# A convolution module whose transfers are put in the source's order

## The chip, the core and the metric

The kernel runs on one core of a Trainium2 chip. The core has engines that run side by side and wait for each other by semaphores: TensorE (PE, matrix products, with its weight loads PEld), VectorE (DVE), ScalarE (ACT), GpSimd (POOL) and SyncE (SP). In this kernel SP issues all transfers between the chip's memory (HBM) and the core's own memory, and 16 DMA engines carry them out. SP runs one instruction stream: a transfer whose wait isn't over holds back all that stand behind it. The metric is the device time of one execution in microseconds, compared by medians.

## What is computed

Two layers of a diffusion trunk for 256 tokens of width 1024, in float32: layer 0 mixes an mLSTM with differential attention and ends in a SwiGLU; layer 1 is a Conformer convolution module and a SwiGLU with 8 experts, of which each token takes 2. The change is in the convolution module:

```
u = modulate(x, mix_pre_g, sh_m, sc_m)
a, g = jnp.split(u @ pw1_w + pw1_b, 2, axis=-1)
h = a * jax.nn.sigmoid(g)
h = depthwise_conv(h, dw_w) + dw_b          # 31 taps along the tokens
h = jax.nn.silu(layernorm(h, ln_g, ln_b))
y = h @ pw2_w + pw2_b
```

## The kernel before

Activations lie channel-major: 1024 channels are 8 tiles k of 128 partitions, with 256 tokens along the free axis. Weights lie in HBM as units of 128 x 2048 floats, 1 MB each. `raw` loads a unit into a ring of six buffers (four `raw`, two `raw2`), and `half` splits half a unit into a rounded part (`whi`, a cast on ACT, L372) and the rest (`wlo`, a subtraction on DVE, L373), since a float32 product is made of three faster ones. `Ahead` runs these halves ahead of the products.

The module runs over four steps `jj`. A step multiplies two pw1 units, `jj` and `4 + jj` (48 matmuls on PE each), which give tiles 2jj and 2jj+1 of a and of g. One step later `glu` makes h of them (two ACT instructions and one DVE product per tile, L1416 to L1418 before, L1420 to L1422 now) and writes it into `hp`, in the traces one of the buffers `B`. From there the tiles go two ways:

- Tiles 0 and 1 (`NV = 2`) are convolved on DVE: `conv_v` is a generator of 31 steps (L1361 and L1364 before, L1365 and L1368 now), of which `fill(n)` puts n at a time between the other DVE work.
- Tiles 2 to 7 are convolved on PE: `conv(k)` makes 64 matmul records of 32 columns of weights, with the tap weights of a pair of tiles (`taps` units, one for tiles 2 and 3, one for 4 and 5, one for 6 and 7) and with `x4`, four copies of the tile, each shifted by one token. `conv_shift(k)` makes the copies: one write of the tile to scratch in HBM (`hd<-B`, L1345) and four shifted reads (`B<-hd`, L1348). There are three `x4` buffers.

The first two convolved tiles, 0 and 2, give a pilot mean on PE (`mm<-B,on`), which is subtracted from every tile before the sums of the layer norm (`aux<-B,one`, `aux<-m,one`). In program order, inside step 3, PE's row is: product of unit 3, conv(2), pilot, sums, product of unit 7, conv(3), conv(4), conv(5), conv(6), conv(7).

A scheduler orders what isn't bound to the source's order. `order = in_order()` (L1422) binds PE, DVE and ACT for the module, but not SP: SP's transfers come in the order in which the scheduler finds their buffers free and their data ready, and loads of later parts (the pw2 units) are taken in between. The kernel's last part, the experts, streams some 270 MB of weights through the same SP queue.

Of the kernel before, what the change touches and what calls it, by code (L numbers as in the profile page):

```python
# [11 lines left out]
F32 = mybir.dt.float32  # L12
# [7 lines left out]
P = 128  # L20
# [11 lines left out]
HW = T + 32  # L32
# [6 lines left out]
NV = 2  # L39
# [197 lines left out]
def build(ctx: ExitStack, tc: tile.TileContext, d, unit, dbg=None):  # L237
    nc = tc.nc
# [5 lines left out]
    def nm(s):  # L244
        ctr[0] += 1
        return f"{s}_{ctr[0]}"
# [7 lines left out]
    def tl(shape, tag, dt=F32, bufs=1):  # L254
        pool = sb
        for n, tags in (("l0", L0), ("l1", L1)):
            if tag in tags:
                pool, bufs = pools[n], tags[tag]
        return pool.tile(shape, dt, tag=tag, name=nm(tag), bufs=RING.get(tag, bufs))
# [3 lines left out]
    def ring(tag, dt=F32, w=UW):  # L263

        n2 = L1[tag + "2"] if "l1" in pools else 0
        q = pos_[tag] % (RING[tag] + n2)
        pos_[tag] += 1
        return tl([P, w], tag if q < RING[tag] else tag + "2", dt)
# [7 lines left out]
    def pm(tag="mm"):  # L276
        return ps.tile([P, 512], F32, tag=tag, name=nm(tag))
# [3 lines left out]
    def mm(out, lhsT, rhs, start, stop):  # L281
        PE.matmul(out, lhsT, rhs, start=start, stop=stop)  # L282
# [33 lines left out]
    def C(n, a=0, b=None):  # L316
        o, w = COL[n]
        return col[:, o + a : o + (w if b is None else b)]
# [11 lines left out]
    def raw(key, src=None, two=False):  # L330

        src = d["w"][unit[key]] if src is None else src
        tag = room.pop(0) if room else "raw"
        if tag in ("gp", "w", "xn", "pT"):
            if tag == "w":
                t = [ring("whi", F32, HW_), ring("wlo", F32, HW_)]
            else:
                t = [tl([P, HW_], "gp"), tl([P, HW_], "m4")] if tag == "gp" else [tl([P, HW_], tag, bufs=2) for _ in range(2)]
            for q in range(2):
                nc.sync.dma_start(t[q], src[:, HW_ * q : HW_ * q + HW_])  # L340
            return t
        t = ring("raw") if tag == "raw" else tl([P, UW], tag)
        if two:
            for q in range(2):
                nc.sync.dma_start(t[:, HW_ * q : HW_ * q + HW_], src[:, HW_ * q : HW_ * q + HW_])
        else:
            nc.sync.dma_start(t, src)
        return t[:, :HW_], t[:, HW_:]
# [148 lines left out]
    def fill(n=1000):  # L497

        while background and n > 0:
            if next(background[0], 0) == 0:  # L500
                background.pop(0)
            else:
                n -= 1
# [134 lines left out]
    ET = mybir.EngineType  # L638

    def in_order(*engines):  # L640
        return tc.manual_schedule(engines=set(engines or (ET.PE, ET.DVE, ET.Activation)))
# [119 lines left out]
    def wstat(half, out, n0, n1):  # L761
        h, l = by_k(half, KT)
        for k in range(KT):
            mm(out, h[:, k], uh[k][:, n0:n1], k == 0, False)
            mm(out, h[:, k], ul[k][:, n0:n1], False, False)
            mm(out, l[:, k], uh[k][:, n0:n1], False, k == KT - 1)
# [175 lines left out]
    for j2 in range(2):  # L942
        W = split(("dk", j2))
        for j in range(2):
# [4 lines left out]
            ks = tl([P, S], "cv", bufs=2)[:, :T]  # L949
# [223 lines left out]
    with in_order():  # L1173
# [17 lines left out]
        for n in range(8):  # L1191
            i, t = n // 2, n % 2
# [141 lines left out]
    hp = tl([P, 7, HW], "B8")  # L1334
    G.memset(hp, 0.0)
    hp = [hp[:, k, :] for k in range(7)] + [hp[:, 3, :]]
    b2 = tl([P, 16], "b2")
    V.tensor_scalar(b2, C("pw1b"), 0.5, None, ALU.mult)
    x4s = [tl([P, 4, HW - 4], "B8") for _ in range(3)]
    cvo = tl([P, KT, T], "B8")  # L1340


    def conv_shift(k):
        hd = hdram.tile([P, HW], F32, tag="hd", name=nm("hd"), bufs=4)
        nc.sync.dma_start(hd, hp[k])  # L1345
        x4 = x4s[k % 3]
        for j in range(4):
            nc.sync.dma_start(x4[32 * j : 32 * j + 32], hd[:, j : j + HW - 4].rearrange("(c p) t -> p c t", c=4))  # L1348

    def conv(k):  # L1350
        w4 = w4s[k // 2][k % 2].rearrange("p (b c) -> p b c", c=32)
        x4 = x4s[k % 3]
        pk = pm("mm")
        for q in range(8):
            for c in range(4):
                mm(pk[32 * c : 32 * c + 32, :T], w4[:, 8 * c + q, :], x4[:, c, 4 * q : 4 * q + T], q == 0, q == 7)
        convolved(k, pk[:, :T], C("dwb", k, k + 1))
# [23 lines left out]
    def convolved(k, src, bias):  # L1381

        o = cvo[:, k, :]
        n = len(done)
        done.append(k)
        if n >= 2:
            if bias is None:
                V.tensor_tensor(o, src, pilot, ALU.subtract)
            else:
                V.scalar_tensor_tensor(o, src, bias, pilot, ALU.add, ALU.subtract)  # L1390
            pend.append((n, k))
            return
        if bias is not None:
            A.activation(o, src, AF.Identity, bias=bias)
        if n == 2 - 1:
            pmu = pm("mm")
            for m, k in enumerate(done):
                mm(pmu[:, :T], on, cvo[:, k, :], m == 0, m == 2 - 1)
            A.copy(pilot, pmu[:, :T])
            for m, k in enumerate(done):  # L1400
                V.tensor_tensor(cvo[:, k, :], cvo[:, k, :], pilot, ALU.subtract)
                sums(m, k)

    pend = []
    w4s = {}

    def drain(n=0):
        while len(pend) > n:
            sums(*pend.pop(0))

    hdram = ctx.enter_context(tc.tile_pool(name="hdram", bufs=1, space=bass.MemoryType.DRAM))
    def glu(jj, pp):
        for j in range(2):
            k = 2 * jj + j
            s = tl([P, 512], "cv", bufs=2)[:, :T]
            A.activation(s, pp[1][:, T * j : T * j + T], AF.Tanh, bias=b2[:, 8 + k : 9 + k], scale=0.5)  # L1416
            A.activation(s, s, AF.Copy, bias=0.5, scale=0.5)
            V.scalar_tensor_tensor(hp[k][:, 15 : 15 + T], pp[0][:, T * j : T * j + T], C("pw1b", k, k + 1), s, ALU.add, ALU.mult)  # L1418
            if k < NV:
                background.append(conv_v(k))  # L1420

    order = in_order()  # L1422
    order.__enter__()
    pp = None
    for jj in range(4):
        if jj >= NV // 2:
            w4s[jj] = raw(("taps", jj))
        prev, pp = pp, []
        for n in (jj, 4 + jj):
            p_ = pm("mm")  # L1430
            for j in range(2):
                ahead.step()
                wstat(ahead.get(("pw1", n), j), p_[:, T * j : T * j + T], 0, T)
                if prev:
                    glu(jj - 1, prev)
                    if jj > 1:
                        conv_shift(2 * jj - 2)
                    if jj != 3 and jj > 1:
                        conv_shift(2 * jj - 1)
                    prev = None  # L1440
                    fill(2)
                else:
                    fill(4)
            pp.append(p_)
            fence.close()
            if jj == 3 and n == jj:
                conv(2)
                drain(2)
                conv_shift(5)
    conv(3)  # L1450
    drain(2)
    glu(3, pp)
# [57 lines left out]
    for q in (1, 0):  # L1510
        for t in range(TT):
            j = TT * q + t
# [816 lines left out]
```

## Time and profile before

| | us |
|---|---|
| median of 3 runs (1305.63 to 1310.74) | 1307.46 |
| the profiled execution | 1306.39 |
| its span | 1304.4 |
| PE busy | 1243.8 (95%) |
| DVE busy | 641.1 (49%) |
| ACT busy | 439.8 (34%) |

406.42 MB are moved, 312 GB/s in the mean. Starts are microseconds from the span's start. PE's products of the module start at about 473 us and the last sums end at about 555 us; the experts run from about 600 us. A row of a timeline merges instructions of one kind, with their count behind the x; in brackets stand the idle time before it and what ended it. "DMA to landing" is the time from the issue on SP to the semaphore that tells the data is there.

### The profile page before, as it was taken

The numbers are of one execution on the slowest core, as the hardware profiler recorded it, in microseconds if no ns is written. First come the engines' busy times: TensorE is split into PE (matmuls) and PEld (weight loads), VectorE is DVE, ScalarE is ACT, GpSimd is POOL, SyncE is SP. The second block draws the span as 40 slices with busy tenths as digits, with TensorE's granted clock in tenths as the row PEclk, the third lists the DMA queues.
The fourth block names the chain that finished last, engine by engine and source line by source line (L and its number), as shares of the span: only waits on it lengthen the run. The fifth ranks groups of instructions, "written<-read, shape, count | busy, mean of one in ns | idle before, by whom it ended". The sixth has DMA issues, their size and how long they took to land. (4 is left out here: it accounts for less than half of the span.)

```text
span 1304.4 us, 22683 instructions
## 1 busy us (share of the span) xinstructions
PE 1243.8 (95%) x9234; PEld 798.8 (61%) x9234; DVE 641.1 (49%) x1065; ACT 439.8 (34%) x800; POOL 32.7 (3%) x83
## 2 busy tenths in 40 slices
PE   6999999989999998999999699999999999999996
PEld 4878776788998988576444343444433434678532
DVE  4589758698887658653212112111121121699422
ACT  4553247563444554253121010210011102577311
POOL 1000001100000010000100000000000000000000
PEclk9999999999999999999999899999999999999998
DMA  8728830468988616687869999999999997999994
GB/s 337 285 95 298 308 127 1 162 269 347 369 338 325 255 72 198 190 304 275 326 265 413 420 419 419 419 421 394 364 420 421 419 397 275 426 359 369 356 413 193
DMA packets 71091, 406.42 MB, mean 312 GB/s; under 512 B 7875, under 2 KB 12227, under 8 KB 31813
## 3 DMA queue, kind: packets, MB, share of 16 engines
q1 hardware_dynamic: 70980, 404.91, 79.1%
q8 instruction: 74, 1.21, 0.4%
q14 instruction: 37, 0.29, 0.1%
HBM read 402.94 MB, written 1.93 MB: 310 GB/s over the span
## 5 line engine op out<-in xcount | busy, mean ns | idle before, releaser
L373 DVE TENSOR_TENSOR wlo<-raw,whi 128x1024 fp32r<-128x1024 f32 x154 | 185.8, 1222 | 46.7 <-ACT whi L372 46.1
L282 PE MATMUL mm<-raw,gL 128*32 128x256 f32 (+3 forms) x1392 | 195.1, 439 | 5.5 <-DMA raw<-w 5.5
L372 ACT CAST whi<-raw 128x1024 fp32r<-128x1024 f32 x154 | 159.1, 1048 | 96.4 <-PE mm L282 62.0
L282 PE MATMUL mm<-B,whi 128*128 128x256 f32 x960 | 171.7, 282 | 0.2 <-DVE B L632 0.2
L282 PEld LDWEIGHTS mm<-B,whi 128*128 128x128 f32 x960 | 148.3, 189 | 2.3 <-PE mm L282 0.6
L282 PE MATMUL mm<-B,wlo 128*128 128x256 f32 x480 | 134.9, 281 | 0.0
L282 PEld LDWEIGHTS mm<-raw,gL 128*32 128x32 f32 (+1 forms) x1392 | 77.1, 122 | 83.1 <-issue 58.5
L282 PE MATMUL mm<-B,gL 128*32 128x256 f32 (+3 forms) x808 | 124.3, 448 | 3.8 <-DMA B<-w 3.8
L1893 DVE TENSOR_TENSOR cv<-cv,mm 64x512 f32<-64x512 f32 (+1 forms) x36 | 23.3, 647 | 205.5 <-ACT cv L1892 205.3
L1892 ACT ACTIVATE cv<-mm 64x512 f32<-64x512 f32 (+1 forms) x36 | 19.9, 554 | 256.6 <-PE mm L282 256.5
L282 PE MATMUL aux<-whi,pT 128*128 128x512 f32 (+2 forms) x400 | 100.9, 425 | 2.4 <-DVE pT L1909 1.8
L282 PEld LDWEIGHTS mm<-B,wlo 128*128 128x128 f32 x480 | 90.5, 189 | 0.0
L282 PEld LDWEIGHTS mm<-B,gL 128*32 128x32 f32 (+1 forms) x808 | 46.7, 122 | 56.8 <-issue 42.6
L282 PE MATMUL aux<-raw,pT 128*32 128x256 f32 (+1 forms) x592 | 78.2, 472 | 0.5 <-DMA raw<-w 0.5
L282 PE MATMUL aux<-wlo,pT 128*32 128x256 f32 (+2 forms) x284 | 69.4, 430 | 2.0 <-DVE wlo L373 1.1
L282 PEld LDWEIGHTS aux<-whi,pT 128*128 128x128 f32 (+2 forms) x400 | 49.3, 158 | 26.8 <-issue 12.5
L282 PE MATMUL mm<-U,whi 128*128 128x256 f32 (+1 forms) x240 | 64.5, 331 | 0.0
L1909 DVE COPY pT<-aux 128x384 f32<-128x384 f32 (+4 forms) x42 | 19.0, 453 | 91.9 <-PE aux L1902 83.5
L282 PE MATMUL aux<-B,pT 128*32 128x256 f32 (+2 forms) x424 | 58.6, 455 | 0.6 <-DMA B<-w 0.6
L282 PE MATMUL mm<-whi,B 128*128 128x512 f32 (+1 forms) x192 | 58.0, 377 | 0.0
L282 PE MATMUL mm<-whi,gL 128*32 128x256 f32 (+3 forms) x336 | 55.0, 455 | 2.3 <-DMA whi<-w 2.3
L282 PE MATMUL mm<-wlo,gL 128*32 128x256 f32 (+3 forms) x336 | 54.2, 452 | 0.0
(467 smaller groups left out, 1867.3 us busy)
## 6 DMA issues: line engine op xcount, KB each, us to landing
raw<-w SPq DMA_DIRECT2D x237, 1024.0 KB, 7.3
B<-w SPq DMA_DIRECT2D x69, 1024.0 KB, 11.2
whi<-w SPq DMA_DIRECT2D x52, 512.0 KB, 11.3
wlo<-w SPq DMA_DIRECT2D x52, 512.0 KB, 11.1
gp<-w SPq DMA_DIRECT2D x18, 512.0 KB, 10.1
m<-w SPq DMA_DIRECT2D x18, 512.0 KB, 10.0
B<-hd SPq DMA_DIRECT2D x24, 142.0 KB, 5.2
x<-x SPq DMA_DIRECT2D x2, 512.0 KB, 5.0
```

The lines of the kernel that those rows point to most:

```text
L282: PE.matmul(out, lhsT, rhs, start=start, stop=stop)
L372: A.copy(hi, rq)
L373: V.tensor_tensor(lo, rq, f(hi), ALU.subtract)
L1892: A.activation(s, p_[:64, :w], AF.Silu)
L1893: V.tensor_tensor(s, s, p_[64:, :w], ALU.mult)
L1909: V.tensor_copy(h[:, :o], pt[:, :o])
```

## The change

`in_order` takes SP in as well, so all transfers of the module go out in the order of the source (loads of later parts may still stand between them). `conv_shift` takes several tiles: first all scratch writes, then all reads. The load of a step's taps moves from the step's start to its end.

```diff
-    def conv_shift(k):
-        hd = hdram.tile([P, HW], F32, tag="hd", name=nm("hd"), bufs=4)
-        nc.sync.dma_start(hd, hp[k])
-        x4 = x4s[k % 3]
-        for j in range(4):
-            nc.sync.dma_start(x4[32 * j : 32 * j + 32], hd[:, j : j + HW - 4].rearrange("(c p) t -> p c t", c=4))
+    def conv_shift(*ks):
+        hds = []
+        for k in ks:
+            hd = hdram.tile([P, HW], F32, tag="hd", name=nm("hd"), bufs=4)
+            nc.sync.dma_start(hd, hp[k])
+            hds.append(hd)
+        for k, hd in zip(ks, hds):
+            x4 = x4s[k % 3]
+            for j in range(4):
+                nc.sync.dma_start(x4[32 * j : 32 * j + 32], hd[:, j : j + HW - 4].rearrange("(c p) t -> p c t", c=4))
...
-    order = in_order()
+    order = in_order(ET.PE, ET.DVE, ET.Activation, ET.SP)
     order.__enter__()
     pp = None
     for jj in range(4):
-        if jj >= NV // 2:
-            w4s[jj] = raw(("taps", jj))
         prev, pp = pp, []
         for n in (jj, 4 + jj):
...
                     if jj > 1:
-                        conv_shift(2 * jj - 2)
-                    if jj != 3 and jj > 1:
-                        conv_shift(2 * jj - 1)
+                        conv_shift(*range(2 * jj - 2, 2 * jj - (jj == 3)))
...
                 conv_shift(5)
+        if jj >= NV // 2:
+            w4s[jj] = raw(("taps", jj))
     conv(3)
```

PE's order of instructions stays as it was. On SP, around the first scratch writes, there stood before (raw_4705, raw_917_4847 and raw_4995 are the three taps units, raw_4746, raw_914_4813 and raw_4900 the pw1 units 6, 3 and 7, raw_5514 and raw_986_5583 pw2 units, hd_4886 and hd_4892 the scratch of tiles 2 and 3):

```order
L347 DMA raw_4675<-w 128x2048
L347 DMA raw_4705<-w 128x2048
L347 DMA raw_4746<-w 128x2048
L347 DMA raw_914_4813<-w 128x2048
L1460 DMA pT_5223<-pb 1x1024 x2
L347 DMA raw_917_4847<-w 128x2048
L347 DMA raw_4900<-w 128x2048
L347 DMA raw_4995<-w 128x2048
L347 DMA raw_5514<-w 128x2048
L347 DMA raw_986_5583<-w 128x2048
L1345 DMA hd_4886<-B_882_4572 128x288
L1345 DMA hd_4892<-B_882_4572 128x288
```

Now (raw_4744, raw_4811 and raw_924_4898 are the pw1 units 6, 3 and 7, raw_916_4845 and raw_4993 the first two taps units):

```order
L347 DMA raw_4675<-w 128x2048
L347 DMA raw_4744<-w 128x2048
L347 DMA raw_4811<-w 128x2048
L347 DMA raw_916_4845<-w 128x2048
L1347 DMA hd_4884<-B_882_4572 128x288
L1347 DMA hd_4886<-B_882_4572 128x288
L1352 DMA B_886_4578<-hd_4884 32x4x284 x4
L1352 DMA B_884_4576<-hd_4886 32x4x284 x4
L347 DMA raw_924_4898<-w 128x2048
L347 DMA raw_4993<-w 128x2048
L347 DMA raw_986_5583<-w 128x2048
L1347 DMA hd_5028<-B_882_4572 128x288
```

Five units stood ahead of the first scratch write that now stand behind the eight reads of its pair or later; pw1 unit 7 is the first of them.

On SP at the end of the module there stood before (hd_5217 and hd_5275 are the scratch of tiles 6 and 7, raw_993_5595 a pw2 unit):

```order
L1345 DMA hd_5217<-B_882_4572 128x288
L1345 DMA hd_5275<-B_882_4572 128x288
L347 DMA raw_993_5595<-w 128x2048
L1348 DMA B_884_4576<-hd_5217 32x4x284 x4
L1348 DMA B_885_4577<-hd_5275 32x4x284 x4
```

Now (raw_5514, raw_5526 and raw_993_5595 are pw2 units):

```order
L1347 DMA hd_5217<-B_882_4572 128x288
L347 DMA raw_5514<-w 128x2048
L1352 DMA B_884_4576<-hd_5217 32x4x284 x4
L1462 DMA pT_5223<-pb 1x1024 x2
L1347 DMA hd_5275<-B_882_4572 128x288
L347 DMA raw_5526<-w 128x2048
L1352 DMA B_885_4577<-hd_5275 32x4x284 x4
L347 DMA raw_993_5595<-w 128x2048
```

The two writes stood together ahead of all eight reads; now write, reads, write, reads, with a weight unit behind each write.

On DVE, from glu(1) to the end of conv_v(0), there stood before (wlo_4903 and wlo_4936 are the halves of pw1 unit 7, wlo_5517 and wlo_5521 those of a pw2 unit, the L1418 rows are glu(2)):

```order
L1364 SCALAR_TENSOR_TENSOR B_887_4579<-B_882_4572,col_68,B_887_4579 128x256 x2
L373 TENSOR_TENSOR wlo_4903<-raw_4900,whi_4902 128x1024
L1364 SCALAR_TENSOR_TENSOR B_887_4579<-B_882_4572,col_68,B_887_4579 128x256 x4
L373 TENSOR_TENSOR wlo_4936<-raw_4900,whi_4935 128x1024
L1364 SCALAR_TENSOR_TENSOR B_887_4579<-B_882_4572,col_68,B_887_4579 128x256 x3
L373 TENSOR_TENSOR wlo_5517<-raw_5514,whi_5516 128x1024
L1364 SCALAR_TENSOR_TENSOR B_887_4579<-B_882_4572,col_68,B_887_4579 128x256 x4
L373 TENSOR_TENSOR wlo_5521<-raw_5514,whi_5520 128x1024
L1364 SCALAR_TENSOR_TENSOR B_887_4579<-B_882_4572,col_68,B_887_4579 128x256
L1418 SCALAR_TENSOR_TENSOR B_882_4572<-mm_4849,col_68,cv_5022 128x256
L1418 SCALAR_TENSOR_TENSOR B_882_4572<-mm_4849,col_68,cv_5026 128x256
L1364 SCALAR_TENSOR_TENSOR B_887_4579<-B_882_4572,col_68,B_887_4579 128x256 x3
```

Now (wlo_4901 and wlo_4934 are the halves of pw1 unit 7):

```order
L1368 SCALAR_TENSOR_TENSOR B_887_4579<-B_882_4572,col_68,B_887_4579 128x256 x2
L373 TENSOR_TENSOR wlo_4901<-raw_924_4898,whi_4900 128x1024
L1368 SCALAR_TENSOR_TENSOR B_887_4579<-B_882_4572,col_68,B_887_4579 128x256 x4
L373 TENSOR_TENSOR wlo_4934<-raw_924_4898,whi_4933 128x1024
L1368 SCALAR_TENSOR_TENSOR B_887_4579<-B_882_4572,col_68,B_887_4579 128x256 x8
L1422 SCALAR_TENSOR_TENSOR B_882_4572<-mm_4847,col_68,cv_5020 128x256
L1422 SCALAR_TENSOR_TENSOR B_882_4572<-mm_4847,col_68,cv_5024 128x256
L1368 SCALAR_TENSOR_TENSOR B_887_4579<-B_882_4572,col_68,B_887_4579 128x256 x3
```

The pw2 halves are gone from here; they and the second pw2 unit's halves stand further back, between the results of conv(5) and conv(6), and the conv_v steps run on without them.

## Rows read from the trace of the kernel before

**Rows 1.** Waits of PE, 500 to 560 us: waiting, releaser, total, times, longest
```profile
PE mm L282 <- DMA B<-hd: 5.4, 2, 4.0
```

**Rows 2.** Timeline of PE, 512 to 562 us: start, duration, instruction, count, idle before
```profile
513.16 0.27 PE L282 MATMUL mm<-B,wlo 128*128 128x256 f32 x1
517.40 5.20 PE L282 MATMUL mm<-B,raw 128*32 128x256 f32 x64 [3.97 <-DMA B<-hd]
522.53 1.36 PE L282 MATMUL mm<-B,on 128*128 128x256 f32 x4
...
526.15 0.51 PE L282 MATMUL mm<-B,whi 128*128 128x256 f32 x2
...
532.02 10.57 PE L282 MATMUL mm<-B,raw 128*32 128x256 f32 x192
...
546.13 3.66 PE L282 MATMUL mm<-B,raw 128*32 128x256 f32 x64 [1.47 <-DMA B<-hd]
...
549.86 3.55 PE L282 MATMUL mm<-B,raw 128*32 128x256 f32 x58
```

**Rows 3.** Windows: busy of PE, PEld, DVE, ACT, POOL; PE clock, DMA share, GB/s
```profile
519.00:520.00 1.00, 1.00 (x16) 0.51 (x12) 0.96 (x3) 0.00 (x0) 0.00 (x0) 0.50 1.13 315
...
521.00:522.00 1.00, 1.00 (x25) 0.59 (x21) 0.00 (x0) 0.00 (x0) 0.00 (x0) 1.00 1.01 360
```

**Rows 4.** Timeline of SP, 478 to 562 us
```profile
481.61 23.85 SPq L347 DMA_DIRECT2D raw<-w  x5
505.57 0.84 SPq L1345 DMA_DIRECT2D hd<-B  x2
512.69 3.66 SPq L1348 DMA_DIRECT2D B<-hd  x8
...
518.43 0.40 SPq L347 DMA_DIRECT2D raw<-w  x1
...
536.66 0.81 SPq L1345 DMA_DIRECT2D hd<-B  x2
537.56 0.41 SPq L347 DMA_DIRECT2D raw<-w  x1
538.47 5.06 SPq L1348 DMA_DIRECT2D B<-hd  x8
```

**Rows 5.** Timeline of DVE, windows 505.4 to 513 and 512 to 562 us
```profile
505.02 0.87 DVE L1418 SCALAR_TENSOR_TENSOR B<-mm,col,cv 128x256 f32<-128x256 f32 x2
...
506.72 1.22 DVE L373 TENSOR_TENSOR wlo<-raw,whi 128x1024 fp32r<-128x1024 f32 x1
...
510.95 1.52 DVE L1364 SCALAR_TENSOR_TENSOR B<-B,col,B 128x256 f32<-128x256 f32 x3
...
517.01 0.87 DVE L1418 SCALAR_TENSOR_TENSOR B<-mm,col,cv 128x256 f32<-128x256 f32 x2
517.80 1.52 DVE L1364 SCALAR_TENSOR_TENSOR B<-B,col,B 128x256 f32<-128x256 f32 x3
...
525.01 4.12 DVE L1364 SCALAR_TENSOR_TENSOR B<-B,col,B 128x256 f32<-128x256 f32 x8
```

**Rows 6.** Landing of the scratch write issued at 505.57
```profile
DMA to landing us min/median/max: 7.1/7.1/7.1
```

**Rows 7.** Landing of the eight reads issued from 512.69 on
```profile
DMA to landing us min/median/max: 2.8/3.3/3.8
```

**Rows 8.** Landing of the eleven weight units issued from 481.6 to 554.1
```profile
DMA to landing us min/median/max: 4.7/5.6/7.8
```

**Rows 9.** Landing of the weight unit issued at 518.43
```profile
DMA to landing us min/median/max: 5.7/5.7/5.7
```

**Rows 10.** Timeline of ACT, 480 to 562 us: the cast of unit 7's first half
```profile
504.84 1.05 ACT L372 CAST whi<-raw 128x1024 fp32r<-128x1024 f32 x1 [0.15 <-PE mm L282]
```

**Rows 11.** Waits of SP's queue, 596 to 640 us
```profile
SPq L347 <- PE mm L282: 28.4, 3, 18.2
```

**Rows 12.** The windows view, 740 to 760 us
```profile
740.00:760.00 20.00, 13.15 (x163) 7.27 (x155) 1.23 (x4) 0.65 (x2) 0.00 (x0) 0.84 1.01 425
```

## Prediction

> **What bounds the kernel now.** I read, in this order, PE's waits in the convolution module, PE's timeline there, the SP timeline, the landings of single DMAs, and DVE's timeline. Over the whole run PE is the busiest engine, and in the module (473 to 560 us) it has almost no gaps: of its waits there the reader is to see one of weight, 5.4 us in two pieces on `B<-hd`, the shifted reads [rows 1]. The larger piece stands in front of conv(2): the last pw1 product of unit n=3 starts at 513.16, and conv(2) starts at 517.40 after 3.97 us of idling; the smaller, 1.47 us, stands in front of conv(6) at 546.13 [rows 2]. The first piece has a second price: conv(2)'s 64 matmuls take 5.20 us where conv(6)'s 64 take 3.66, because the granted clock is 0.50 (1.2 GHz) after the idling and 1.00 again at 521 [rows 2, 3].
>
> Why the reads are late stands on SP. Five weight units are issued from 481.61 on; the last has just gone out when the scratch writes of tiles 2 and 3 follow at 505.57 [rows 4], right after their data: the two DVE products of glu(1) start at 505.02 [rows 5]. The first write takes 7.1 us to land [rows 6], and the first read goes out at 512.69. For the later pair the first read follows its write (536.66) after 1.81 us [rows 4]. The difference is the 1 MB unit issued 0.4 us ahead of the write.
>
> **What the change removes.** The order of PE is the same before and after. On SP the taps load moves behind its step, the pw2 units no longer float ahead of the scratch writes, and everything on SP now stands in source order. Up to glu(1) the DVE and ACT orders are the same, so the scratch writes still go out at 505.57. With no weight unit ahead of them I take 1.8 us to land: first read at 507.4. Eight reads take 3.66 us to issue, 0.46 apart [rows 4], so the fourth goes out at 508.8 and, with the 3.3 us of the eight reads of before [rows 7], lands at 512.1. PE comes at 513.4, so the 3.97 us go, and with them the slow clock: conv(2) would end at 513.4 + 3.66 = 517.1 instead of 522.6, a gain of 5.5 us if nothing else were late.
>
> **What it adds: a late weight unit, and an idle engine behind it.** Something else is late. Unit 7 of pw1 (raw_4900 before, raw_924_4898 now) is needed by the ACT cast and the DVE subtraction that stand right behind glu(1) in both orders. Before, SP issued it among the five from 481.61 on. Now it stands behind the two scratch writes and eight reads, and SP waits in front of the first write until glu(1) is done, although the buffer for unit 7 is free. So it is issued at 507.4 + 3.66 = 511.1. Landing from there: single units took 4.7 to 7.8 us, median 5.6 [rows 8]; the one issued at 518.43, 2 us after eight reads and behind two writes, took 5.7 [rows 9]. I take 5.7, the nearest case: 516.8, bounds 515.8 and 518.9. (The Trainium skill, page DMA: Bandwidth & Descriptors, section Anatomy of one DMA, gives for the GpSimd-issued path about 2.0 us plus bytes over 436 GB/s, 4.4 us for 1 MB; here no unit took less than 4.7 [rows 8], and by the page the sum below would be 1.3 us smaller. I go by the row.)
>
> Behind the landing DVE works in order. Cast 1.05 us [rows 10] with 0.1 to start: the subtraction starts at 518.0 instead of 506.72. From there to the start of the run of conv_v steps behind the second half's subtraction it is 4.23 us, as before (510.95 - 506.72): 522.2. Then come eight steps in one run where before there were 3 + 4 + 1 with the two halves of a pw2 unit between them: 4.12 us as in the row of eight, 526.3. Then glu(2), 0.79 to the next start, 527.1, and three steps, 1.52: conv_v(0) is complete at 528.6. Before it was complete at 517.80 + 1.52 = 519.3 [rows 5]. The two subtractions that moved away are already out of this: they give back 2.0 of the 11.3 us.
>
> This is where PE stands. After conv(2) its next work is the pilot mean, which reads conv_v(0) and conv(2); unit 7's product comes after that. Before, conv(2) was last there and the pilot started at 522.53; now conv(2) ends at 517.1 and the pilot waits for DVE until 528.6, an idle of 11.5 us where there was one of 3.97. The pilot's four matmuls took 1.36 us, at full clock [rows 2]; after this idle I reckon them at half clock, 1.9. From their end (522.53 + 1.36 = 523.9) to the product at 526.15 it was 2.26 us; with the sums at half clock I reckon 2.8. So the product starts at 533.3 instead of 526.15, 7.1 late, and I add 0.6 for its own first part at half clock: **7.7 us late** at 532.02, the end of it. Bounds: an early landing and full clock throughout give 5.0; a late landing and a clock that stays low for 4 us give 10.4.
>
> **The second pair of the module, at its end.** conv(3) to conv(5) find their data landed: the writes of tiles 4 and 5 go out behind glu(2) at 526.8 and 531, more than 10 us before use. The write of tile 6 waits for glu(3), as before, so it shifts with PE. What changes is tile 7. Before, both writes went out together (536.66), and all eight reads in one run [rows 4]. Now write 6, a weight unit, four reads, two small loads, write 7, another unit, four reads: write 7 goes out 4 us later, and lands behind the unit and the first reads; conv(6) started on those at 546.13, so I put it at 546.3. Its four reads follow until 547.7. To land, a fourth read took 3.3 us alone [rows 7] and 6.1 behind a unit just issued (from 540.0, the fourth of the reads from 538.47 on, to 546.13) [rows 2, 4]; the unit here is under way for 3 us by then, so I take 4.3: 552.0, where conv(7) started at 549.86 [rows 2]. All these plus the 7.7. So **2.1 us more**, bounds 1.1 and 3.9. The two pw2 splits, now behind conv(5)'s result on DVE, 4 x 1.22 us [rows 5], fit before conv(7)'s result, and cost nothing; if conv(7) were not late, they would cost up to 2.
>
> **Downstream.** Two pw2 units and the first expert units are issued 9 to 12 us later. Cover: SP later stood 18.2 us with all buffers full, waiting for PE at one DMA [rows 11], so the weight stream has room to catch up. Behind that wait every issue is set by a buffer that PE frees, so PE's lateness passes to the end: cost of the later loads 0, price of PE's lateness in full.
>
> **Sum.** 1306.39 us for the profiled execution (span 1304.4 and 2.0 around it) + 7.7 + 2.1 = **1316.2**. Bounds of the two terms: 6.1 to 14.3 more, 1312.5 to 1320.7. The profiled execution lies 1.1 under the median of the runs shown, 1307.46, which I leave as the scatter of the runs.
>
> **Rivals.**
> - *Made up later (0.14).* PE starves for weights: in 740 to 760 us it is busy for 13.15 of 20 us with the DMA engines full [rows 12]. If the weight stream isn't shifted, a late PE just idles less there, and 10 us vanish: about 1307.5. Against it: the 18.2 us wait, which ties the stream to PE before that.
> - *Only the gain counts (0.08), the other side.* If unit 7 is there when DVE wants it, the early conv(2) is worth 5.5 us: 1300.9. It decides by the landing: conv_v(0) is complete 11.8 us after it, so for no loss against 522.53 the unit must land by 510.8, for the whole gain by 505.3. That needs an issue that doesn't wait behind glu(1). (The Trainium skill, page DMA: Bandwidth & Descriptors, section Anatomy of one DMA, has every semaphore wait happen on the issuing sequencer before dispatch; the trace agrees, with the first read held on SP from 506.4 to 512.69 [rows 4].)
> - *More is late (0.12).* The last pw2 units, issued after conv(7)'s reads, hold up the pw2 products at 562 us: two units of 1 MB behind each other, 5 us on top, 1321.
>
> **How the numbers follow.** The forecast has 0.66 with its own range 1312 to 1320.5. Down to 1309 and up to 1321 the range holds all but the gain case, the fully absorbed one and a thin upper tail. What a measurement can tell from no change is 0.5%, 6.5 us, so against the median of the runs slower begins at 1314.0. Of the forecast's 0.66 some 0.10 lies under that. Slower 0.56 + 0.12 = 0.68; same 0.14 + 0.10 + 0.01 = 0.25; faster 0.07.
>
> **What would show it.** Right: no PE wait on the reads before conv(2); unit 7 issued on SP at about 511; DVE idle some 11 us in front of the first subtraction behind glu(1); PE idle 11 us between conv(2) and the pilot, the clock at 0.50 after it; conv(7) waiting for `B<-hd` about 2 us; and then the same pattern about 10 us later, to the end. Wrong: unit 7 issued before 505, DVE not idle there, or the lateness gone by 760 us.

## The result: 1.0 % slower, and the profile after

The changed kernel takes 1321.85 us (median of 6 runs, 1318.87 to 1326.0) where the kernel before takes 1308.89 (6 runs, 1305.63 to 1311.88): ratio 1.0100, 95% interval 1.0081 to 1.0118, 13.0 us more. The forecast was 1316.2, range 1309 to 1321: slower as forecast, and by more than the range holds. The profiled execution of the changed kernel is its slowest, 1326.0 us (span 1324.2).

PE's waits in the module, 500 to 560 us, in answer to [rows 1] (waiting engine, releaser: total, times, longest):

```profile
PE mm L282 <- DVE B L1368: 14.3, 1, 14.3
PE mm L282 <- DMA B<-hd: 1.1, 1, 1.1
```

The 4.0 us in front of conv(2) is gone, and 14.3 us on DVE, on the conv_v steps that the pilot reads, stand in its place. PE's timeline, in answer to [rows 2], from conv(2) to conv(7):

```profile
512.97 3.66 PE L282 MATMUL mm<-B,raw 128*32 128x256 f32 x64
...
530.97 2.05 PE L282 MATMUL mm<-B,on 128*128 128x256 f32 x4 [14.34 <-DVE B L1368]
...
535.71 0.80 PE L282 MATMUL mm<-B,whi 128*128 128x256 f32 x2
...
543.30 10.57 PE L282 MATMUL mm<-B,raw 128*32 128x256 f32 x192
...
556.98 3.66 PE L282 MATMUL mm<-B,raw 128*32 128x256 f32 x64 [1.05 <-DMA B<-hd]
...
563.50 5.30 PE L282 MATMUL mm<-B,raw 128*32 128x256 f32 x64 [2.32 <-DMA B<-hd]
```

conv(2) starts without a wait and at the full clock (3.66 us, not 5.20). The pilot starts at 530.97 instead of 522.53, unit 7's product at 535.71 instead of 526.15, conv(3) at 543.30 instead of 532.02: 11.3 us late. conv(7) is 13.6 us late and takes 5.30 us. The windows, in answer to [rows 3] (busy time of PE, PEld, DVE, ACT, POOL, then PE's granted clock, DMA share, GB/s):

```profile
518.00:519.00 1.00, 0.00 (x0) 0.00 (x0) 0.00 (x0) 0.00 (x0) 0.00 (x0) 1.00 0.72 303
...
530.00:531.00 1.00, 0.04 (x1) 0.07 (x1) 0.96 (x3) 0.00 (x0) 0.00 (x0) 0.50 0.29 104
538.00:539.00 1.00, 1.00 (x6) 1.00 (x6) 0.26 (x1) 0.00 (x0) 0.00 (x0) 0.50 0.60 150
...
540.00:541.00 1.00, 1.00 (x11) 1.00 (x10) 0.00 (x0) 0.00 (x0) 0.00 (x0) 1.00 0.80 140
```

PE stops at 516.6; the granted clock is still 1.00 at 518, 0.50 when the pilot runs, and 0.50 through the first half of unit 7's product: PE's count in a microsecond is 6 at 538 and 11 at 540. The queue of SP, in answer to [rows 4]:

```profile
505.17 0.81 SPq L1347 DMA_DIRECT2D hd<-B  x2
507.06 4.07 SPq L1352 DMA_DIRECT2D B<-hd  x8
511.23 13.69 SPq L347 DMA_DIRECT2D raw<-w  x3
...
547.93 0.34 SPq L1347 DMA_DIRECT2D hd<-B  x1
548.31 0.51 SPq L347 DMA_DIRECT2D raw<-w  x1
549.79 1.79 SPq L1352 DMA_DIRECT2D B<-hd  x4
551.63 0.61 SPq L1462 DMA_DIRECT2D pT<-pb  x2
552.29 0.35 SPq L1347 DMA_DIRECT2D hd<-B  x1
554.18 0.35 SPq L347 DMA_DIRECT2D raw<-w  x1
557.13 1.76 SPq L1352 DMA_DIRECT2D B<-hd  x4
```

The first write and the first read are 1.9 us apart, not 7.1 [rows 4, 6]. Unit 7 is the first of the three loads at 511.23. It lands at the upper end of my bounds, not near the 5.7 us that I had taken:

```profile
DMA to landing us min/median/max: 7.8/7.8/7.8
```

ACT's cast of it, in answer to [rows 10], and DVE's row behind it, in answer to [rows 5], show who waits for that landing (the DVE steps of L1368 need nothing of unit 7; they stand behind it in DVE's order, and no run moved them):

```profile
519.16 1.99 ACT L372 CAST whi<-raw 128x1024 fp32r<-128x1024 f32 x2 [14.87 <-DMA raw<-w]
```

```profile
520.24 1.23 DVE L373 TENSOR_TENSOR wlo<-raw,whi 128x1024 fp32r<-128x1024 f32 x1 [13.84 <-ACT whi L372]
...
524.47 4.13 DVE L1368 SCALAR_TENSOR_TENSOR B<-B,col,B 128x256 f32<-128x256 f32 x8
528.51 0.87 DVE L1422 SCALAR_TENSOR_TENSOR B<-mm,col,cv 128x256 f32<-128x256 f32 x2
529.30 1.52 DVE L1368 SCALAR_TENSOR_TENSOR B<-B,col,B 128x256 f32<-128x256 f32 x3
```

To compare executions whose clocks start differently I measure the module from the first row of glu(0) on DVE to the first MAX8 of the routing: 99.7 us before (492.86 to 592.54), 116.9 after:

```profile
492.46 0.98 DVE L1422 SCALAR_TENSOR_TENSOR B<-mm,col,cv 128x256 f32<-128x256 f32 x2
...
609.34 0.17 DVE L1592 MAX8 mx<-lg 128x8 f32<-128x8 f32 x1
```

So the module is 17.2 us longer in these two executions, the slowest of the six of the changed kernel and one 2.5 us under the median of the kernel before. Nothing of it is made up: from the routing's rank row to the end it is 674.3 us before and 674.7 after.

### The profile page after: what moved, and what is told of

It is laid out like the page before. It is cut to its first block, busy times and chain, and to the rows that moved or that the text cites. A ratio compares the mean times of both kernels' runs of the same rounds, so it can differ in the third digit from the quotient of the medians.

```text
span 1324.2 us, 22673 instructions
## 1 busy us (share of the span) xinstructions
PE 1252.4 (95%) x9234; PEld 805.2 (61%) x9234; DVE 641.3 (48%) x1065; ACT 438.9 (33%) x800; POOL 32.6 (2%) x83
## 5 line engine op out<-in xcount | busy, mean ns | idle before, releaser
L1895 DVE TENSOR_TENSOR cv<-cv,mm 64x512 f32<-64x512 f32 (+1 forms) x36 | 23.3, 647 | 206.5 <-ACT cv L1894 206.3
L282 PEld LDWEIGHTS mm<-B,gL 128*32 128x32 f32 (+1 forms) x808 | 46.7, 123 | 56.9 <-issue 42.7
## 6 DMA issues: line engine op xcount, KB each, us to landing
B<-w SPq DMA_DIRECT2D x69, 1024.0 KB, 11.3
whi<-w SPq DMA_DIRECT2D x52, 512.0 KB, 11.7
wlo<-w SPq DMA_DIRECT2D x52, 512.0 KB, 11.1
```

The costliest lines, as they stand in the source:

```text
L1895: V.tensor_tensor(s, s, p_[64:, :w], ALU.mult)
```

## The experiments

Two theories stood at the start: **the late unit** (SP in source order puts unit 7 behind the shift; DVE, the pilot and PE wait for it), and **the bound queue itself** (any order that SP must keep costs, wherever the unit stands). Medians are beside those of the kernel before on the same chip; "module" is the length just defined, of one profiled execution.

| kernel | median us | before | ratio, 95% interval | module us |
|---|---|---|---|---|
| changed | 1321.85 | 1308.89 | 1.0081 to 1.0118 | 116.9, 117.9, 115.6, 111.3 |
| E1 unit 7 first | 1316.33 | 1308.85 | 1.0029 to 1.0073 | 103.9 |
| E2 PE kept busy | 1320.64 | 1308.85 | 1.0056 to 1.0118 | 111.6 |
| E3 SP free | 1308.96 | 1308.85 | 0.9972 to 1.0003 | 101.4 |
| E4 SP's order alone | 1332.11 | 1308.85 | 1.0120 to 1.0198 | 119.5 |
| E6 unit 7 between | 1328.44 | 1309.72 | 1.0113 to 1.0182 | 118.2 |
| E7 units placed | 1312.11 | 1309.72 | 0.9998 to 1.0037 | 98.7 |
| E8 write 7 with 6 | 1322.76 | 1309.72 | 1.0066 to 1.0134 | 112.2 |
| E9 units spread | 1310.73 | 1310.85 | 0.9988 to 1.0020 | 101.2 |
| E10 taps later | 1322.62 | 1310.14 | 1.0072 to 1.0158 | 115.0 |
| E11 spread, one fewer | 1309.56 | 1310.14 | 0.9966 to 1.0005 | 101.3 |
| E12 changed, shift on GpSimd | 1320.33 | 1309.39 | 1.0065 to 1.0108 | 111.5 |
| E13 before, shift on GpSimd | 1321.54 | 1309.39 | 1.0065 to 1.0109 | 111.1 |

**E3 and E4: which part of the change costs.**

```
E3, to the changed kernel:
-    order = in_order(ET.PE, ET.DVE, ET.Activation, ET.SP)
+    order = in_order()
E4, to the kernel before:
-    order = in_order()
+    order = in_order(ET.PE, ET.DVE, ET.Activation, ET.SP)
```

> The changed kernel with SP left out of the order again; the paired scratch writes and the taps load at the step's end stay. Theory (the bound SP queue makes unit 7 late): SP issues unit 7 ahead of the scratch writes again, conv(2) waits some 4 us for its reads as before, and the time is that of before within 3 us, 1306 to 1312. Rival (pairing or the moved taps load is the cause): as slow as the changed kernel, 1319 to 1326.

> The kernel before with SP bound to the source's order, and nothing else: taps load at the step's start, a write and four reads per tile. Theory (the bound SP queue makes unit 7 late): unit 7 stands behind write, reads, write, reads, some 2 to 3 us later than in the changed kernel: 13 to 17 us slower than before, 1322 to 1326. Rival (pairing or the moved taps load is the cause): within 3 us of before.

With SP free the pairing and the moved taps load cost nothing: 1308.96. SP's order alone costs 23.3 us, more than expected: there the pilot waits 16.6 us and conv(2) 3.4. The order is the cause, and the other edits win back some 10 us of it.

**E1: unit 7 ahead of the shift.** Its load is issued before the scratch writes of tiles 2 and 3.

```
+                    if jj == 2:
+                        ahead.load()      # raw(pw1 unit 7) now; step() uses it
                     if jj > 1:
                         conv_shift(*range(2 * jj - 2, 2 * jj - (jj == 3)))
```

> The changed kernel with one transfer moved: pw1 unit 7 is loaded ahead of the scratch writes of tiles 2 and 3, where its buffer is long free. Theory (the late unit 7 is the loss): DVE does not idle behind glu(1), conv_v(0) is complete at about 517, the pilot starts right behind conv(2) at about 517 instead of 531, PE's wait of 14.3 us and the half clock behind it are gone. conv(7) still waits about 2 us for its reads. Against the kernel before: 5.5 us gained at conv(2), 2 to 4 lost at conv(7): 2 to 4 us faster than before, about 1305. Rival (the weight stream as a whole is late, or the end of the module is the loss): still 8 us or more slower than before, 1317 or more.

The first part came as expected: the pilot follows conv(2), 0.4 us of waiting in place of 14.3. PE in this kernel:

```profile
515.18 3.66 PE L282 MATMUL mm<-B,raw 128*32 128x256 f32 x64
519.26 1.10 PE L282 MATMUL mm<-B,on 128*128 128x256 f32 x4 [0.42 <-DVE B L1372]
...
541.28 4.92 PE L282 MATMUL mm<-B,raw 128*32 128x256 f32 x64 [5.68 <-DMA B<-hd]
...
549.18 3.66 PE L282 MATMUL mm<-B,raw 128*32 128x256 f32 x64 [2.54 <-DMA B<-hd]
...
556.08 3.66 PE L282 MATMUL mm<-B,raw 128*32 128x256 f32 x64 [2.81 <-DMA B<-hd]
```

The time is a miss: 7.5 us over before, not under it. conv(5), (6) and (7) now wait 11.0 us for their reads, since pw2 units, which the source does not order, stand between the writes and the reads:

```profile
521.65 0.55 SPq L1351 DMA_DIRECT2D hd<-B  x1
532.21 0.35 SPq L347 DMA_DIRECT2D raw<-w  x1
532.61 2.64 SPq L1356 DMA_DIRECT2D B<-hd  x4
```

The write of tile 5 goes out at 521.65; the load behind it waits until 532.21 for the buffer that conv(3) frees, and the reads wait behind the load. So both theories hold a part: the late unit is the first 14 us wait, and a bound queue hands its holds on to whoever stands behind.

**E7, E9, E11: every load placed.** Built on E1, with the pw2 and MoE loads given places in the source, so that none stands between a write and its reads.

```
E7:
-        if jj >= NV // 2:
-            w4s[jj] = raw(("taps", jj))
+        if jj == 1:
+            w4s[1] = raw(("taps", 1))
+        if jj == 2:                                # behind the reads of 2, 3
+            for j in (2, 3):
+                w4s[j] = raw(("taps", j))
+            for c in range(2):
+                ready2[c, 0] = raw(("pw2", c, 0))  # used by Out.split
...
+    scratch(6)
+    scratch(7)
     conv_shift(6)
...
     conv_shift(7)
+    for c in range(2):
+        ready2[c, 1] = raw(("pw2", c, 1))
...
     conv(7)
+    for k in (("m1", 0, 0, 0), ("m3", 0, 0, 0), ("m1", 0, 0, 1)):
+        pre[k] = raw(k)
E9: taps 3 and pw2 (0,0), (0,1) behind the reads of 4, 5; pw2 (1,0), (1,1) behind 7
E11: taps 3 and pw2 (0,0) behind the reads of 4, 5; pw2 (1,0), (0,1), (1,1) behind 7
```

> The changed kernel with every weight load of the module given a place in the source, so that none floats between a scratch write and its reads: pw1 unit 7 ahead of the writes of tiles 2 and 3; both tap units and two pw2 units behind their reads; the write of tile 7 beside that of tile 6; the other two pw2 units behind the reads of tile 7; the three MoE units behind conv(7). Theory A (the loss is only what stands in the bound queue at the wrong place): the waits of the products on shifted reads, 11.0 us in the kernel with unit 7 first, go to under 3, no product of the module waits for the late unit, and the time is 1300 to 1306, faster than both kernels. Theory B (a bound queue costs by itself, each held DMA delays what is behind it, wherever it stands): a new wait comes in place of the old ones, 1310 to 1320.

> As the kernel with every unit placed, but the loads spread: behind the reads of tiles 2 and 3 only tap unit 2; tap unit 3 and the pw2 units of the first column half behind the reads of tile 5; the pw2 units of the second half behind the reads of tile 7. Theory A (in that kernel four 1 MB loads in a row, issued 514 to 516, stood ahead of tile 4's scratch write at 518.4, whose reads were issued only at 531, and so conv(4), (5) and (6) waited 2.5, 1.6 and 0.9 us, and the last sums 2.2 us for the second pw2 unit): these waits go, reads of tile 4 are issued by 523, the module ends 4 to 7 us earlier, and the time is 1304 to 1308, faster than before by 0.1 to 0.4 %. Theory B (the loads only move, and the MoE units that now start later are late in their turn): waits appear behind the module, and the time stays at 1310 to 1314.

> The kernel with the loads spread, with one pw2 unit instead of two behind the reads of tile 5, and the three others behind the reads of tile 7. Theory A (there the scratch writes of tiles 6 and 7, issued at 531.2 behind three 1 MB loads of 525 to 526, landed only at 538.8, and conv(6) waited 4.3 us): behind two loads they land by 536, conv(6) waits under 1.5 us at the full clock, the module from the first glu to the MAX8 takes 95 to 98 us (before 99.3 to 99.7), and the time is 1305 to 1309, 0.1 to 0.4 % below before. Theory B (the pw2 and MoE units loaded later are then what the products wait for): the module is as short, and the stretch behind it longer by as much, 1310 to 1313.

E7 leaves 2.4 us of the 13.0 and E9 none, but no version beats the kernel before: E7 and E9 miss what was expected, and E11's 1309.56 cannot be told from no change. In E9 conv(2) to conv(5) have no wait, and the gain is given back at conv(6):

```profile
526.57 10.57 PE L282 MATMUL mm<-B,raw 128*32 128x256 f32 x192
...
543.48 6.08 PE L282 MATMUL mm<-B,raw 128*32 128x256 f32 x64 [4.26 <-DMA B<-hd]
```

Its scratch write was issued at 531.2, 38.4 us behind glu(0) (43.8 in the kernel before), but 5 us behind three 1 MB loads, and landed in 7.5 us. E11 has two loads there, and still 7.0 us and a wait of 3.73: that expectation fell. A write with no load ahead lands in 1.8. The packets of the DMA queue show the order. A row of a weight unit makes a packet of 8 KB, a row of a scratch write one of 1.1 KB. In the kernel before, from 505.6 to 509, behind the first scratch write's issue at 505.57, only packets of the load move; from 511 to 512.7, when that write lands, only the last few small ones:

```profile
DMA packets 97, 0.79 MB, mean 234 GB/s; under 512 B 0, under 2 KB 0, under 8 KB 0
...
DMA packets 14, 0.01 MB, mean 7 GB/s; under 512 B 4, under 2 KB 14, under 8 KB 14
```

**E6, E10: why unit 7 lands late.** E6 issues it between the writes and the reads; E10 moves the tap load, which the changed kernel issues 0.4 us behind it, to the reads of tile 5.

```
E6:  +                    if jj == 2:
     +                        scratch(2, 3); ahead.load()
E10:                  conv_shift(5)
     +                w4s[2] = raw(("taps", 2))
     -        if jj >= NV // 2:
     +        if jj >= NV // 2 and jj != 2:
```

> The changed kernel with pw1 unit 7 loaded between the scratch writes of tiles 2 and 3 and their eight reads, not behind the reads. Theory A (the late start of unit 7's product is the landing time of its load, and this grows behind the eight reads): issued at about 507 us it lands in 5 to 6 us, by 513, the pilot follows conv(2) without the 14.3 us wait and unit 7's product starts before 525 (changed kernel 535.7); the reads start some 0.5 us later and land slower, so conv(2) starts 1 to 4 us later than 512.9. The time is that of the kernel with the unit ahead of the writes, about 1316, since the same later units then stand between writes and reads of tiles 4 and 5. Theory B (the landing does not depend on what is ahead of it): the same 7.8 us, landed at 515, and still nothing of the wait left at the pilot; what tells the two apart is the landing time of that load, 5 to 6 or 7.8.

> The changed kernel with the load of tap unit 2, which it issues right behind pw1 unit 7, moved behind the reads of tile 5. Theory A (unit 7 lands in 7.8 instead of 5.7 us since the next 1 MB load is issued 0.4 us behind it and shares the DMA engines): alone it lands in 5.2 to 6.2 us, its first cast starts at 516.5 to 517.5 on the changed kernel's clock of the first glu, the pilot waits 12 us instead of 14.3, and the time falls by 1.5 to 3 us. Theory B (the eight reads ahead of it make it late): it still lands in 7.3 to 8.3 us and the time is the changed kernel's.

E10 settles the neighbour: alone behind the reads the unit still takes 7.5 us, and the time does not move. E6 is a miss on both sides: 6.9 us with the reads behind it, 5.6 us of waiting left at the pilot, 2.5 at conv(2), 13.1 in all for shifted reads, and 18.7 us over the kernel before. What the unit waits for is seen in the changed kernel's own windows (the last two columns):

```profile
509.00:510.00 1.00, 1.00 (x11) 1.00 (x10) 0.00 (x0) 0.00 (x0) 0.00 (x0) 1.00 0.85 241
...
512.00:513.00 1.00, 1.00 (x13) 0.87 (x13) 0.00 (x0) 0.00 (x0) 0.00 (x0) 1.00 1.10 229
...
517.00:518.00 1.00, 0.00 (x0) 0.00 (x0) 0.00 (x0) 0.00 (x0) 0.00 (x0) 1.00 1.03 434
```

The DMA engines are full from 509 on, at 229 to 247 GB/s while the eight reads run, and reach 434 GB/s only when the unit loads are alone. The reads move 1.16 MB (two tiles of 128 x 4 x 284 x 4 bytes), 4.9 us at 235 GB/s, and unit 7 is issued 0.5 us behind the last of them. The packets show that it follows that work: from its issue to 512.8, for 1.6 us, no packet of 8 KB moves (first row; in E10 the first moves 2.0 us behind the issue, and for a unit with nothing ahead, issued at 507.2 in E12, 1.0 us behind it). At the other end, in E10 from 516.5 until the unit lands at 518.8, only its last 16 packets move, and the 16 DMA engines are busy for 13.8% (last two rows), the work of about two engines:

```profile
DMA packets 343, 0.35 MB, mean 230 GB/s; under 512 B 39, under 2 KB 343, under 8 KB 343
...
DMA packets 24, 0.13 MB, mean 57 GB/s; under 512 B 8, under 2 KB 8, under 8 KB 8
q1 hardware_dynamic: 24, 0.13, 13.8%
```

So the reads hold the unit's start back, and a few late packets set its end. Why these are late is not shown, and no kernel took the reads away, so their share of the 7.8 us isn't measured.

**E12, E13: a queue of its own for the shift.**

```
-            nc.sync.dma_start(hd, hp[k])       # and the four reads
+            nc.gpsimd.dma_start(hd, hp[k])
```

> The changed kernel with the scratch writes and the shifted reads issued on GpSimd's queue instead of SyncE's; the source order of SyncE's queue stays, and now it holds the weight loads alone. Theory A (the loss is head-of-line waiting: a weight load that stands behind the shift in one queue): unit 7's load is issued when its buffer is free, before 507, its first cast no longer waits for it, the pilot follows conv(2), and the time falls below 1312, if the issue on GpSimd is not dear. Theory B (the loss is the DMA engines' work itself, whichever queue issues it: 7.6 us for a load among small copies): the unit is still late by several us and the time stays above 1316. A price not known from the runs so far: what one issue on GpSimd takes; eight reads are 16 x 0.5 us on SyncE, and above 1 us each on GpSimd conv(2) would wait for them.

> The kernel before with the same edit: writes and reads of the shift on GpSimd's queue, SyncE unordered as before. Theory A (in the kernel before conv(2) waits 4.0 us since its scratch write stands 0.4 us behind a 1 MB load, and not since SyncE's queue holds it): the write still lands late and conv(2) still waits 3 to 5 us; 1306 to 1311, the same as before. Theory B (the queue holds it): conv(2) waits under 1 us at the full clock, and the time falls by 3 to 6 us, to 1303 to 1306.

In E12 unit 7 is on time, with 0.0 us of waiting at the pilot, and the time hardly falls (1320.33): the wait moved to the reads, 11.7 us in two pieces. (The expectation counts 16 issues for eight reads; they are eight.) GpSimd's timeline and PE's:

```profile
508.24 1.38 POOL L1347 DMA_DIRECT2D hd<-B  x2 [35.54 <-DVE B L1422]
515.04 4.38 POOL L1352 DMA_DIRECT2D B<-hd  x8 [5.43 <-DMA hd<-B]
```

```profile
521.35 6.46 PE L282 MATMUL mm<-B,raw 128*32 128x256 f32 x64 [5.78 <-DMA B<-hd]
```

E13, the control, loses 12 us on the kernel before, which neither theory had: conv(2) waits 6.1 us there and conv(6) 8.0. Issuing is not dear (4.38 us for eight reads, 3.66 on SP); the write takes 6.1 to 6.5 us to land on a queue where nothing is ahead of it but a unit on the other queue, issued 1 us before, and 7.1 to 7.9 for the later pairs. So a queue of its own does not cure it: E12's theory A holds for the unit and falls for the time, and E13's theory B fell. Where the write's time goes in E12 is seen in the packets from 508.3 to 511, 511 to 512 and 513 to 514 (q1 is SP's queue, q0 GpSimd's; the last column is the share of 16 engines):

```profile
DMA packets 101, 0.83 MB, mean 306 GB/s; under 512 B 0, under 2 KB 0, under 8 KB 0
...
q1 hardware_dynamic: 33, 0.16, 43.6%
q0 software_dynamic: 46, 0.17, 41.7%
...
q0 software_dynamic: 2, 0.01, 4.7%
```

Until 511, 2.8 us behind the write's issue, only packets of 8 KB move, those of the load. From 511 to 512 both queues move about as much, and the write's last packets go out one by one until it lands, with the engines nearly idle. (The Trainium skill, page DMA: Bandwidth & Descriptors, section Queues, rings and completion order, has each DMA engine take turns between the queues that have work. The trace agrees for 511 to 512, with 0.16 and 0.17 MB side by side, and shows no turn of the write before 511.) Whether the load or the issue on GpSimd keeps the write's first packets back stays open: no write was issued there far from any load.

**E2, E8: the clock and the end of the module.** E2 lets PE run 58 dummy matmuls in the wait before the pilot; E8 issues tile 7's write beside tile 6's.

```
E2:  +            warm(58, "aux")
                  pmu = pm("mm")
E8:       glu(3, pp)
     +    scratch(6, 7)
```

> The changed kernel with 58 matmuls without use between conv(2) and the pilot, some 12.4 us at full clock, into PE's wait. Theory (a part of the loss is the half clock behind the wait, not the wait): the granted clock stays 1.00 through pilot, sums and unit 7's product, which gives back 0.7 + 0.6 + 1.9, some 3 us: about 10 us slower than before instead of 13. Rival (the wait alone): the time of the changed kernel, 13 us slower than before, or more if the matmuls outlast the wait.

> The changed kernel with the scratch write of tile 7 issued beside that of tile 6, and nothing else. Theory A (the last 4 us of the loss are conv(7)'s wait for its reads, 2.3 us, and the half clock behind it, 1.6 us): conv(7) starts without a wait at the full clock, and the time falls by 2 to 4 us to 1318 to 1320. Theory B (the end of the module is not on the path that sets the time): no change, 1321.9.

E2 keeps the granted clock (mean 0.984 instead of 0.972; pilot 1.10 us), and conv(3) starts 47.8 us behind glu(0) instead of 50.8; yet its median, 1320.64 against 1321.85, is within the scatter: the 3 us are seen in the module and not in the time. E8 removes conv(7)'s wait as expected (it starts at 561.11 without one), yet the median stays at 1322.76. Its module is 4.7 us shorter than that of the changed kernel's profiled execution, so either that execution was not typical or the gain was lost behind. The next runs bear on it.

**The two kernels again.** Three more profiled executions of the changed kernel, one of the kernel before.

> The changed kernel unchanged, for a second profiled execution: the one shown was its slowest, 4.2 us over the median. Theory A (the module's loss is the same in each execution, and the stretch from the routing's first MAX8 to the ranks, 40.2 us there and 37.6 in the kernel before, varies): from the first glu to the MAX8 116 to 118 us, and another length of that stretch. Theory B (the half clock at the end of the module, conv(7) at 5.30 us, is not there in each execution): 112 to 115 us, conv(7) at 3.7 us.

> The kernel before unchanged, for a second profiled execution. Theory A: from the first glu to the MAX8 99.7 us within 1 us, as shown, and from there to the ranks another length than 37.6 us, up to 43. Theory B (the module varies too): 98 to 103 us.

> The changed kernel unchanged, a third profiled execution. Two profiled executions took 1326.0 and 1325.9 us with 116.9 and 117.9 us from the first glu to the MAX8; the six timed ones have a median of 1321.85. Theory A (the module's end differs between executions): an execution near 1320 shows conv(7) without the half clock, 3.7 us, and 112 to 114 us to the MAX8. Theory B (the difference lies ahead of the module or behind it): 116 to 118 us again, whatever the time.

> As the third profiled execution of the changed kernel, with the same two theories: near 1320 us with conv(7) at 3.7 us and 112 to 114 us from the first glu to the MAX8, or 116 to 118 us again.

They took 1325.9, 1326.05 and 1321.04 us; before 1307.93, module 99.3. The fourth, 0.8 us under the median, is near what the first theory of these runs said: module 111.3 us (112 to 114 expected), conv(7) at the full clock:

```profile
541.61 10.57 PE L282 MATMUL mm<-B,raw 128*32 128x256 f32 x192
...
561.19 3.66 PE L282 MATMUL mm<-B,raw 128*32 128x256 f32 x64 [1.56 <-DMA B<-hd]
```

In the three longer executions conv(7) waits 2.3 to 3.2 us and then takes 5.3 to 6.3; here it waits 1.56 and takes 3.66. Wait and clock together set 2 to 4 us between executions. The length of the one wait does not decide on the clock: E1's conv(6) and conv(7) waited 2.5 and 2.8 us and ran at the full one. Unit 7's landing varies too: 7.8, 7.5, 7.0 and 6.1 us. What E8 takes away is thus often not there.

## Why the prediction had its steps right and its sizes too small

The chain of waits came as forecast. What failed is sizes: the landing and the half clock inside the 7.7 us at conv(3), and the base of the sum.

- *What the change removes*: right. conv(2) starts directly behind the last product, at the full clock.
- *Unit 7 issued at 511.1*: 511.23. Counted from glu(0), which starts 0.4 us earlier in this execution, it is 0.5 us late: the eight reads took 4.07 us to issue, not 3.66.
- *Landing 5.7, bounds 4.7 to 7.8*: **the first term that was too small**, though inside its bounds. It took 7.8 us in the profiled execution, 6.1 to 7.8 in four; 2.1 us of the shortfall there, 0.4 in the execution near the median. I had taken the one unit at 518.43 as the nearest case [rows 9] because it too stood behind reads; those had been issued 2 us before it, these 0.5 us.
- *DVE behind the landing*: right to 0.2 us. From the start of the first subtraction to the run of eight steps 4.23 us, then 4.13, 0.79 and 1.52; the pilot starts 2.4 us later than forecast (530.97, 528.6), of which the landing is 2.1.
- *Pilot to product*: forecast 4.7 us, measured 4.74.
- *"0.6 for its own first part at half clock"*: **the second term that was too small, and the one that left its bounds.** The clock was at 0.50 until 539.6, for half of the product and not its first part alone: product to conv(3) 7.59 us, forecast 6.4. From the pilot to conv(3) it was 11.9 to 12.3 us in all four executions, forecast 11.1. Counted from glu(0), conv(3) is 11.7 us late against 7.7: 0.5 from the issue, 2.1 from the landing, 1.2 from this clock, where my upper bound, 10.4, had the 2.1 and 0.6. In the fourth execution, near the median, it is 9.8 (48.96 us from glu(0) against 39.16), inside the bounds.
- *2.1 us more at conv(7)*: right as a wait, 13.6 - 11.3 = 2.3. That the half clock comes back behind it, 5.30 instead of 3.66 us, was not in the sum, though the same pattern stood in front of conv(2) in the profile of before [rows 2, 3]. In the fourth execution this second price is absent.
- *Downstream in full*: right. SP still stood 20.8 us waiting for PE at one DMA, in answer to [rows 11], and the stretch of [rows 12] is there again 20 us later (12.79 of 20 us busy in 760 to 780):

```profile
SPq L347 <- PE mm L282: 22.6, 3, 20.8
```

- *The rivals*: "made up later" fell (674.3 and 674.7 us behind the ranks). "Only the gain counts" fell, and E1 shows its condition: with unit 7 on time the pilot follows conv(2). "More is late" fell; no pw2 unit held a product up.
- *The sum*: **its base failed too.** I added to one execution of the kernel before, 1306.39 us, and left its distance from the median, 1.1 us by the three runs then shown, as scatter. The median of six is 1308.89, so 2.5 of the 5.7 us between 1316.2 and 1321.85 are the base; on the median the bounds of my two terms end at 1323.2, not 1320.7, and the measured time is inside. The other 3.2 us are terms: 13.0 measured between the medians, 9.8 forecast. On the execution near the median the module is 11.6 us longer at the MAX8, which gives 1.8 of them; the last 1.4 us are not located. Another 2.6 us of that execution lie between the MAX8 and the ranks (40.2 us there, 37.6 before) and are not shown to belong to the change: that stretch took 37.6, 40.2 and 42.7 in other executions of the changed kernel, and 41.0 in E3, whose median is that of before.

## What to carry to other kernels

When a queue is put in source order, list for each DMA that is bound what it now stands behind, and for each such wait who else is queued there: here a load whose buffer was free waited for data that had nothing to do with it, and E1 shows that moving it only passes the hold on until every load, the unordered ones too, has a place. Take the landing of a load from a case with the same traffic right ahead of it, price each PE wait twice, as the wait and as the half clock that can follow it, and add to the median of the kernel before, not to the one execution that was profiled. A small scratch copy landed fast here only with no large load just ahead of it on its queue; on another queue, beside a load, it was late as well.

## What the runs showed of the hardware that I had not expected

- A scratch write of 0.15 MB landed in 1.8 us with no load ahead (the second of a pair in 3.6), in 7.0 to 7.6 us behind two or three 1 MB loads issued 4 to 6 us before on the same queue (E9, E11), and in 6.0 to 6.5 us on GpSimd's queue behind a load on SP's (E12, E13).
- A landing came with a few last packets while most DMA engines had no work: 13.8% busy in the last 2.3 us of unit 7's load in E10, 3.5% in the last 1.7 us of the scratch write in the kernel before.
- The granted clock came back late: at 0.50 from the pilot at 530.97, with PE busy but for 0.9 us, to 539.6 in the changed kernel, but after the 3.97 us wait of the kernel before it was 1.00 again about 3.2 us after conv(2) began (0.71 in 520 to 521) [rows 2, 3].
- Executions of one program differ by 7 us (1318.87 to 1326.05 for the changed kernel), and two profiles of it differ by up to 6.6 us in the module alone; a difference of a few us between single profiles, as in E8, says little.
